# Splitting the gate weights of a top-2 dispatch by group: the second group's logits and weights moved

## The chip, the cores and the metric

One Trainium2 chip, one of its cores. The time is device microseconds of one execution, median of three runs: 240.18 us (239.93 to 241.43). No matrix work is done; what matters are the 16 DMA engines of the core, which carry all transfers, VectorE, a little of ScalarE, and the two queues from which transfers are issued (SyncE's and ScalarE's).

## The reference

For 16 x 1024 = 16384 tokens there is a row `x` of 512 floats and a row of 8 router logits. The softmax over the 8 is taken, the two largest probabilities are kept and divided by their sum, and the output holds each token's row twice, times the smaller and times the larger weight.

```python
probs = np.exp(router_logits - logits_max)
probs = probs / np.sum(probs, axis=-1, keepdims=True)
topk_indices = np.argsort(probs, axis=-1)[..., -k:]
topk_probs = np.take_along_axis(probs, topk_indices, axis=-1)
topk_probs = topk_probs / np.sum(topk_probs, axis=-1, keepdims=True)
x_expanded = x[:, :, np.newaxis, :].repeat(k, axis=2)
return (x_expanded * topk_probs[..., np.newaxis]).astype(np.float32)
```

All is float32. `x` is 33.6 MB, the logits 0.5 MB, the output 67.1 MB.

## The kernel before, in words

**Tiling.** A token is a row; the tokens are cut into two groups, 65 and 63 rows for each of the 128 partitions (`GROUPS`, L42). In each partition a group's rows are contiguous in memory, so a load of n rows is 128 pieces of n x 2 KB, and a store of n rows 128 pieces of n x 4 KB.

**Memory.** Four tiles of one buffer each: `xs` (65 rows of 512), into which rows are loaded and, once used, products are written too; `osp` (18 double rows), which holds only products; `WA` with the two weights of all 128 rows, and `dlt`. The weights' scratch and the logits lie in `osp` too (`room`, L102 to 107), before it takes its first product.

**Weights.** With two kept probabilities that are divided by their sum, the weights are the sigmoid of minus and plus the difference of the two largest logits. `top2_weights` (L14 to 38) finds the two largest with a tournament of maxima and minima: two steps on VectorE that pair logits 0 to 3 with 4 to 7 (L26, L27), four that halve this (L31 to 34), four that halve it again, and the difference (L36). ScalarE then takes two sigmoids (L37, L38) into `WA`. In the kernel before it is called once, for all 128 rows, so its VectorE steps are 512, 256 and 128 elements wide per partition.

**Order.** Everything is written out by hand, and transfers are kept in the order of the program on their queue. SyncE's queue issues for the first group loads of 2 and 4 rows, then the two groups' logits (L130 for 260 KB, L131 for 252 KB), then loads of 28 and 31 rows (`LOADS`, L44; issued at L122). The products (L138) follow in the order of `STORES` (L47): one `tensor_tensor` on VectorE multiplies n rows, each read twice, with their weights; it goes to `osp` or over rows of `xs` that have been used. Behind each product its store is issued (L151): the very first, of 3 rows, from ScalarE's queue, all others from SyncE's. The product that comes back to the start of `osp` is cut in two (`again`, `FREE`, L136 and 137), so that its first part waits for the small first store alone. The loads of the second group (16, 16 and 31 rows) stand in SyncE's queue behind the last store of the first group; each of them waits until the store that reads its place in `xs` is done. A last instruction of SyncE (L155) waits for the weights, the last product, and all transfers in `moved` but the last.

Of the kernel before, what the change touches and what calls it, by code (L numbers as in the profile page):

```python
# [1 line left out]

# [4 lines left out]

F32 = mybir.dt.float32
ALU = mybir.AluOpType
ACTF = mybir.ActivationFunctionType  # L10
P = 128


def top2_weights(nc, WA, dlt, room, logits, E):  # L14

    tt = nc.vector.tensor_tensor
    hi, lo, n = None, None, E  # L20
    while n > 1:
        n //= 2
        if hi is None:
            a, b = logits[:, :, 0:n], logits[:, :, n : 2 * n]
            nhi, nlo = room(n), b
            tt(nhi, a, b, op=ALU.max)  # L26
            tt(nlo, a, b, op=ALU.min)  # L27
        else:
            a, b = hi[:, :, 0:n], hi[:, :, n : 2 * n]
            nhi, nlo, tmp = room(n), room(n), room(n)  # L30
            tt(tmp, lo[:, :, 0:n], lo[:, :, n : 2 * n], op=ALU.max)  # L31
            tt(nlo, a, b, op=ALU.min)  # L32
            tt(nlo, nlo, tmp, op=ALU.max)  # L33
            tt(nhi, a, b, op=ALU.max)  # L34
        hi, lo = nhi, nlo
    tt(dlt, hi[:, :, 0], lo[:, :, 0], op=ALU.subtract)  # L36
    nc.scalar.activation(WA[:, :, 0], dlt, ACTF.Sigmoid, scale=-1.0)  # L37
    return nc.scalar.activation(WA[:, :, 1], dlt, ACTF.Sigmoid, scale=1.0)  # L38

GROUPS = [65, 63]  # L42

LOADS = [[2, 4, 28, 31], [16, 16, 31]]  # L44
BASE = [0, 1]

STORES = [  # L47
    [(0, 3, "osp", 0), (3, 15, "osp", 3), (18, 16, "xs", 0), (34, 15, "osp", 0), (49, 16, "xs", 33)],
    [(0, 16, "osp", 2), (16, 16, "xs", 0), (32, 15, "osp", 0), (47, 16, "xs", 32)],
]  # L50

L = 18

FREE = [3, 2]


@with_exitstack
def kernel(
    ctx: ExitStack,
    tc: tile.TileContext,  # L60
    x: bass.AP,
    router_logits: bass.AP,
    k: bass.AP,
    out: bass.AP,
):
    nc = tc.nc
    B, S, D = x.shape
    E = router_logits.shape[-1]
    N = B * S
    assert int(k) == 2 and E == 8 and N == P * sum(GROUPS)  # L70
    M = N // P

    x_v, o_v, rl_v = [], [], []
    t0 = 0
    for n in GROUPS:
        t1 = t0 + P * n
        x_v.append(
            x.rearrange("b s d -> (b s) d")[t0:t1].rearrange("(p m) d -> p m d", p=P)
        )
        o_v.append(  # L80
            out.rearrange("b s k d -> (b s) k d")[t0:t1].rearrange(
                "(p m) k d -> p m k d", p=P
            )
        )
        rl_v.append(
            router_logits.rearrange("b s e -> (b s) e")[t0:t1].rearrange(
                "(p m) e -> p m e", p=P
            )
        )
        t0 = t1  # L90

    wpool = ctx.enter_context(tc.tile_pool(name="wpool", bufs=1))
    xs = wpool.tile([P, max(GROUPS), D], F32)
    osp = wpool.tile([P, L, 2, D], F32)
    WA = wpool.tile([P, M, 2], F32)
    dlt = wpool.tile([P, M], F32)


    flat = osp.rearrange("p l k d -> p (l k d)")
    taken = [0]  # L100

    def room(n):  # L102
        o = taken[0]
        taken[0] += M * n
        return flat[:, o : o + M * n].rearrange("p (m n) -> p m n", n=n)

    logits = room(E)

    def place(where, at, n):

        if where == "osp":
            return osp[:, at : at + n]
        return xs[:, at : at + 2 * n, :].rearrange("p (r k) d -> p r k d", k=2)

    moved = []
    m0 = 0
    for g, G in enumerate(GROUPS):
        x0, r = BASE[g], 0
        for n in LOADS[g]:
            moved.append(  # L120
                tc.keep_in_program_order(
                    nc.sync.dma_start(  # L122
                        xs[:, x0 + r : x0 + r + n, :], x_v[g][:, r : r + n, :]
                    )
                )
            )
            r += n
            if g == 0 and r == 6:
                n0 = GROUPS[0]
                tc.keep_in_program_order(nc.sync.dma_start(logits[:, :n0], rl_v[0]))  # L130
                tc.keep_in_program_order(nc.sync.dma_start(logits[:, n0:], rl_v[1]))  # L131
                weights = top2_weights(nc, WA, dlt, room, logits, E)
        assert r == G
        for r, n, where, at in STORES[g]:
            og = place(where, at, n)
            again = where == "osp" and at == 0 and r > 0  # L136
            for a, b in [(0, FREE[g]), (FREE[g], n)] if again else [(0, n)]:
                product = nc.vector.tensor_tensor(  # L138
                    og[:, a:b],
                    xs[:, x0 + r + a : x0 + r + b, :]  # L140
                    .unsqueeze(2)
                    .to_broadcast([P, b - a, 2, D]),
                    WA[:, m0 + r + a : m0 + r + b, :]
                    .unsqueeze(3)
                    .to_broadcast([P, b - a, 2, D]),
                    op=ALU.mult,
                )

            queue = nc.scalar if g == r == 0 else nc.sync
            moved.append(  # L150
                tc.keep_in_program_order(queue.dma_start(o_v[g][:, r : r + n], og))  # L151
            )
        m0 += G

    seen = tc.keep_in_program_order(nc.sync.nop())  # L155
    for ins in [weights, product] + moved[:-1]:
        tc.add_manual_dep(
            seen.ins,
            ins.ins.name,
            mybir.DependencyInfo(  # L160
                mybir.DependencyClass.Sync, mybir.DependencyReason.DATA
            ),
            reason="all but the last transfer is done",
        )


# [1 line left out]
_INS = ['x', 'router_logits', 'k']  # L168
_OUTS = [((16, 1024, 2, 512), 'float32')]

_NUMBERS = {'k': 2}


# [26 lines left out]
```

## Time and profile before

| | before |
|---|---|
| median of three runs | 240.18 us |
| profiled execution, its own time | 241.36 us |
| span of the profiled execution | 239.6 us |
| bytes read, written | 34.08 MB, 67.11 MB |
| VectorE instructions | 22 |
| product of 16 rows (128x16384) | 17,224 ns |
| the weights' VectorE steps, first to last | 8.54 to 12.43 us |

The span runs from the first to the last instruction; the profiled execution's own time is 1.8 us longer. Times within the profile count from the start of the span. A transfer's row gives the time from its issue on the queue to its landing, so the time it stands behind earlier transfers is in it. The DMA share is the mean busy share of the 16 DMA engines; as packets of up to 64 KB are counted where they start, it swings above and below 1 in short windows and is to be read over long ones. "Idle before" an instruction, with the releaser, says for how long its engine stood still and what ended that.

### The profile page before, as it was taken

What the parts mean: (1) busy time and instruction counts of PE and PEld (TensorE: products, weight loads), DVE (VectorE), ACT (ScalarE), POOL (GpSimd) and SP (SyncE); (2) the same over time, 40 slices, a digit from 0 to 9 for tenths busy, and PEclk for the clock granted to TensorE, in tenths of its full rate; (3) what the DMA queues carried; (4) which work ended last, traced back from release to release, by engine and by line L of the source; (5) the groups of instructions that cost most, each with busy time, mean ns of one, the idle gap of its engine ahead of it and who ended that gap; (6) DMA issues with size and microseconds to landing.
All of it is one profiled execution on the core that took longest, in us unless ns stands there. A gap on an engine that the chain in (4) does not pass through costs nothing.

```text
span 239.6 us, 106 instructions
## 1 busy us (share of the span) xinstructions
DVE 141.9 (59%) x22; ACT 1.8 (1%) x3; POOL 0.2 (0%) x4
## 2 busy tenths in 40 slices
DVE  0560499999789999200000699999405999960000
ACT  2000000000000000000000000000000000000000
POOL 0000000000000000000000000000000000000000
DMA  7989998979989897999899999999999899898984
GB/s 253 528 373 483 427 415 376 493 339 492 481 372 492 383 482 339 482 437 449 361 421 438 438 438 498 435 419 471 405 405 471 372 503 442 380 492 360 514 350 186
DMA packets 2592, 101.19 MB, mean 422 GB/s; under 512 B 288, under 2 KB 416, under 8 KB 672
## 3 DMA queue, kind: packets, MB, share of 16 engines
q1 hardware_dynamic: 2448, 99.62, 96.7%
q10 hardware_dynamic: 144, 1.57, 1.5%
HBM read 34.08 MB, written 67.11 MB: 422 GB/s over the span
## 4 chain that ended last, share of the span: by engine, by line
DMA 48%; DVE 40%; SPq 1%; issue 0%; DVEq 0%
DMA xs<-in_x_dram 25%; DVE osp L138 25%; DMA out_dram<-osp 23%; DVE xs L138 14%; SPq L122 0%; SPq L131 0%; SPq L130 0%; SPq L151 0%; DVEq L138 0%
## 5 line engine op out<-in xcount | busy, mean ns | idle before, releaser
L138 DVE TENSOR_TENSOR osp<-xs,WA 128x3072 f32<-128x3072 f32 (+5 forms) x7 | 69.4, 9909 | 62.7 <-DMA xs<-in_x_dram 47.3
L138 DVE TENSOR_TENSOR xs<-xs,WA 128x16384 f32<-128x16384 f32 x4 | 68.9, 17224 | 0.1
L26 DVE TENSOR_TENSOR osp<-osp 128x512 f32<-128x512 f32 x1 | 0.7, 693 | 8.5 <-DMA osp<-in_router_logits_dram 8.5
L37 ACT ACT_TABLE_LOAD x1 | 1.3, 1283 | 0.7 <-PEq L181 0.7
L27 DVE TENSOR_TENSOR osp<-osp 128x512 f32<-128x512 f32 x1 | 0.7, 691 | 0.0
L32 DVE TENSOR_TENSOR osp<-osp 128x256 f32<-128x256 f32 (+1 forms) x2 | 0.7, 351 | 0.0
L31 DVE TENSOR_TENSOR osp<-osp 128x256 f32<-128x256 f32 (+1 forms) x2 | 0.7, 350 | 0.0
L34 DVE TENSOR_TENSOR osp<-osp 128x256 f32<-128x256 f32 (+1 forms) x2 | 0.7, 350 | 0.0
L33 DVE TENSOR_TENSOR osp<-osp 128x256 f32<-128x256 f32 (+1 forms) x2 | 0.7, 350 | 0.0
L37 ACT ACTIVATE WA<-dlt 128x128 f32<-128x128 f32 x1 | 0.3, 315 | 10.5 <-DVE dlt L36 10.5
L36 DVE TENSOR_TENSOR dlt<-osp 128x128 f32<-128x128 f32 x1 | 0.3, 292 | 0.0
L38 ACT ACTIVATE WA<-dlt 128x128 f32<-128x128 f32 x1 | 0.3, 297 | 0.0
L181 POOL MEMSET const-bfloat16-1.0<- 128x1 bf16 x1 | 0.1, 101 | 0.0
L181 POOL MEMSET const-uint8-127<- 128x1 uint8 x1 | 0.1, 101 | 0.0
L181 POOL MEMSET const-float32-0.0<- 128x1 f32 x1 | 0.1, 98 | 0.2 <-issue 0.2
L181 POOL MEMSET const-float32-1.0<- 128x1 f32 x1 | 0.1, 98 | 0.0
## 6 DMA issues: line engine op xcount, KB each, us to landing
out_dram<-osp SPq DMA_DIRECT2D x3, 7680.0 KB, 23.5
xs<-in_x_dram SPq DMA_DIRECT2D x2, 7936.0 KB, 42.2
xs<-in_x_dram SPq DMA_DIRECT2D x2, 4096.0 KB, 40.1
xs<-in_x_dram SPq DMA_DIRECT2D x1, 7168.0 KB, 24.8
out_dram<-osp ACTq DMA_DIRECT2D x1, 1536.0 KB, 26.6
xs<-in_x_dram SPq DMA_DIRECT2D x1, 1024.0 KB, 5.9
xs<-in_x_dram SPq DMA_DIRECT2D x1, 512.0 KB, 3.9
osp<-in_router_logits_dram SPq DMA_DIRECT2D x1, 260.0 KB, 6.2
```

What stands on the lines that cost most here:

```text
L26: tt(nhi, a, b, op=ALU.max)
L27: tt(nlo, a, b, op=ALU.min)
L31: tt(tmp, lo[:, :, 0:n], lo[:, :, n : 2 * n], op=ALU.max)
L32: tt(nlo, a, b, op=ALU.min)
L33: tt(nlo, nlo, tmp, op=ALU.max)
L34: tt(nhi, a, b, op=ALU.max)
L36: tt(dlt, hi[:, :, 0], lo[:, :, 0], op=ALU.subtract)
L37: nc.scalar.activation(WA[:, :, 0], dlt, ACTF.Sigmoid, scale=-1.0)
L38: return nc.scalar.activation(WA[:, :, 1], dlt, ACTF.Sigmoid, scale=1.0)
L138: product = nc.vector.tensor_tensor(og[:, a:b], xs[:, x0 + r + a : x0 + r + b, :] .unsqueeze(2) .to_broadcast([P, b - a, 2, D]), WA[:, m0 ...
L181: nc = _bacc.Bacc("TRN2", target_bir_lowering=False, num_devices=1)
```

## The change

`top2_weights` is called once for each group, on the group's part of `WA` and `dlt`, so its steps are 260, 130 and 65 elements wide for the first group and 252, 126 and 63 for the second. The first group's logits still lie in `osp` and are loaded behind the 2 and 4 rows. The second group's logits go to a tile of their own, `late`, and their load is issued between those of 28 and 31 rows. The second group's weights stand, on VectorE, between the last product of the first group and the first of the second. Their scratch is again the start of `osp`, which the store of rows 34 to 48 of the first group has read before. Each of SyncE's transfers is still there, 18 transfers in all; both logits loads are now in `moved`, and both pairs of sigmoids are waited for at the end.

```diff
+    late = wpool.tile([P, GROUPS[1], E], F32)
     flat = osp.rearrange("p l k d -> p (l k d)")
-    taken = [0]
-
-    def room(n):
-        o = taken[0]
-        taken[0] += M * n
-        return flat[:, o : o + M * n].rearrange("p (m n) -> p m n", n=n)
-
-    logits = room(E)
+    moved, weights = [], []
+
+    def weigh(g):
+
+        n, m = GROUPS[g], sum(GROUPS[:g])
+        taken = [0]
+
+        def room(e):
+            o = taken[0]
+            taken[0] += n * e
+            return flat[:, o : o + n * e].rearrange("p (m n) -> p m n", n=e)
+
+        logits = room(E) if g == 0 else late
+        if g == 0:
+            fetch(g, logits)
+        weights.append(
+            top2_weights(nc, WA[:, m : m + n], dlt[:, m : m + n], room, logits, E)
+        )
+
+    def fetch(g, logits):
+        moved.append(tc.keep_in_program_order(nc.sync.dma_start(logits, rl_v[g])))
...
     for g, G in enumerate(GROUPS):
         x0, r = BASE[g], 0
+        if g == 1:
+            weigh(1)
         for n in LOADS[g]:
...
             r += n
             if g == 0 and r == 6:
-                n0 = GROUPS[0]
-                tc.keep_in_program_order(nc.sync.dma_start(logits[:, :n0], rl_v[0]))
-                tc.keep_in_program_order(nc.sync.dma_start(logits[:, n0:], rl_v[1]))
-                weights = top2_weights(nc, WA, dlt, room, logits, E)
+                weigh(0)
+            if g == 0 and r == 34:
+                fetch(1, late)
...
-    for ins in [weights, product] + moved[:-1]:
+    for ins in weights + [product] + moved[:-1]:
```

More of the change, by code (lines that the diff above doesn't have):

```diff
@@ L113, in place @@
         return xs[:, at : at + 2 * n, :].rearrange("p (r k) d -> p r k d", k=2)
-    moved = []
     m0 = 0
```

## The prediction, before the result was known

> **What bounds the kernel now.** I read the page's first three parts, then windows over the stream of transfers, then the queue's own waits, then the order of time and the transfers one by one. The profiled execution took 241.36 us, its span is 239.6, so 1.8 us lie around it; the median of the three runs shown is 240.18. The sum below is made against the 241.36 and carried over to the median, which lies 1.2 us lower; the changed kernel's time will be a median too.
>
> ```profile
> DVE 141.9 (59%) x22; ACT 1.8 (1%) x3; POOL 0.2 (0%) x4
> DMA packets 2592, 101.19 MB, mean 422 GB/s; under 512 B 288, under 2 KB 416, under 8 KB 672
> q1 hardware_dynamic: 2448, 99.62, 96.7%
> q10 hardware_dynamic: 144, 1.57, 1.5%
> DMA 48%; DVE 40%; SPq 1%; issue 0%; DVEq 0%
> ```
>
> VectorE is busy 59% of the span; the two transfer queues together hold the 16 DMA engines for 98.2% of it. The span windows say where the other 1.8% is:
>
> ```profile
> 0.00:2.00 2.00, 0.00 (x0) 1.28 (x1) 0.20 (x4) 1.00 0.25 31
> 2.00:236.00 234.00, 141.92 (x22) 0.52 (x3) 0.00 (x0) 1.00 1.00 432
> 236.00:239.60 3.60, 0.00 (x0) 0.00 (x0) 0.00 (x0) 1.00 0.04 18
> ```
>
> The last two columns are the DMA share and GB/s. From 2 to 236 us the share is 1.00 at 432 GB/s: 234 us x 432 GB/s = 101.1 MB, all that is moved. Outside there are 2.0 us of start and 3.6 of end. So the time is the bytes over one rate, and the profile's chain of waits, which walks through VectorE for 40% of the span, only shows in what order the stream was fed. A change gains only if it takes bytes or a gap out of the stream, and loses only if it makes one. The test is therefore the cover: how long the stream still has work when the next transfer is issued.
>
> ```profile
> 0.72 0.85 SPq L122 DMA_DIRECT2D xs<-in_x_dram  x2
> 1.62 0.42 SPq L130 DMA_DIRECT2D osp<-in_router_logits_dram  x1
> 2.09 0.43 SPq L131 DMA_DIRECT2D osp<-in_router_logits_dram  x1
> 2.56 1.14 SPq L122 DMA_DIRECT2D xs<-in_x_dram  x2
> 8.54 0.69 DVE L26 TENSOR_TENSOR osp<-osp 128x512 f32<-128x512 f32 x1 [8.54 <-DMA osp<-in_router_logits_dram]
> 12.14 0.29 DVE L36 TENSOR_TENSOR dlt<-osp 128x128 f32<-128x128 f32 x1
> 13.02 3.36 DVE L138 TENSOR_TENSOR osp<-xs,WA 128x3072 f32<-128x3072 f32 x1 [0.58 <-ACT WA L38]
> 16.40 0.37 ACTq L151 DMA_DIRECT2D out_dram<-osp  x1
> 27.42 16.16 DVE L138 TENSOR_TENSOR osp<-xs,WA 128x15360 f32<-128x15360 f32 x1 [11.04 <-DMA xs<-in_x_dram]
> 43.60 0.35 SPq L151 DMA_DIRECT2D out_dram<-osp  x1
> 67.08 12.96 DVE L138 TENSOR_TENSOR osp<-xs,WA 128x12288 f32<-128x12288 f32 x1 [2.98 <-DMA out_dram<-osp]
> 80.07 0.33 SPq L151 DMA_DIRECT2D out_dram<-osp  x1
> 97.33 0.33 SPq L151 DMA_DIRECT2D out_dram<-xs  x1
> 133.58 17.22 DVE L138 TENSOR_TENSOR osp<-xs,WA 128x16384 f32<-128x16384 f32 x1 [36.28 <-DMA xs<-in_x_dram]
> 150.83 0.34 SPq L151 DMA_DIRECT2D out_dram<-osp  x1
> ```
>
> Each row is start and length. The transfers' own rows give KB and us from issue to landing (the first line is the 512 KB load issued at 0.72, the 7680 KB one the store of 43.60, the 24.4 that of 80.07, the 31.2 that of 150.83):
>
> ```profile
> xs<-in_x_dram SPq DMA_DIRECT2D x1, 512.0 KB, 3.9
> osp<-in_router_logits_dram SPq DMA_DIRECT2D x1, 260.0 KB, 6.2
> osp<-in_router_logits_dram SPq DMA_DIRECT2D x1, 252.0 KB, 6.4
> xs<-in_x_dram SPq DMA_DIRECT2D x1, 7168.0 KB, 24.8
> xs<-in_x_dram SPq DMA_DIRECT2D x1, 7936.0 KB, 45.6
> out_dram<-osp ACTq DMA_DIRECT2D x1, 1536.0 KB, 26.6
> out_dram<-osp SPq DMA_DIRECT2D x1, 7680.0 KB, 23.5
> out_dram<-osp SPq DMA_DIRECT2D x1, 7680.0 KB, 24.4
> out_dram<-osp SPq DMA_DIRECT2D x1, 31.2
> ```
>
> The store of 43.60 is the tightest. Its 7.86 MB are 18.2 us at 432 GB/s; it lands after 23.5, so it waited or was in latency for 5.3 us. The 512 KB load, the first in an empty queue, took 3.9 us of which 1.2 are bytes, so an estimate of issue latency plus completion is 2.7. The cover there is 5.3 - 2.7 = 2.6 us; at 80.07 it is 24.4 - 18.2 - 2.7 = 3.5, and at 150.83 (8.39 MB, 19.4 us) 31.2 - 19.4 - 2.7 = 9.1.
>
> **The change part by part.** Logits load of group two, 252 KB, moved from before the 28-row load to behind it. Bytes: the same, 0.26 MB, 0.60 us at 432 GB/s. Ahead of the 28 rows they are gone, so that load's issue goes from 2.56 to about 2.09 and it lands up to 0.6 us sooner. The 31-row load stays the sixth issue of the queue with the same bytes before it, so its landing, and with it the place where stores begin, moves by 0. The target is a new tile, same row length. A small load standing between two large ones is not shown in the trace before; the nearest rows are the two logits loads, which landed at 1.62 + 6.2 = 7.8 and 2.09 + 6.4 = 8.5, 0.7 us apart for 0.60 us of bytes. Bounds: -0.6 (all that the earlier landing could give) to +0.1 beyond the bytes, paid before as well; I take 0.
>
> First group's weights. They wait for one small load, not two: from 8.54 to about 7.8. The chain from 8.54 to the end of L36 at 12.43 takes 3.9 us with widths 512, 256 and 128:
>
> ```profile
> L26 DVE TENSOR_TENSOR osp<-osp 128x512 f32<-128x512 f32 x1 | 0.7, 693 | 8.5 <-DMA osp<-in_router_logits_dram 8.5
> L32 DVE TENSOR_TENSOR osp<-osp 128x256 f32<-128x256 f32 x1 | 0.4, 419 | 0.0
> L32 DVE TENSOR_TENSOR osp<-osp 128x128 f32<-128x128 f32 x1 | 0.3, 283 | 0.0
> L37 ACT ACTIVATE WA<-dlt 128x128 f32<-128x128 f32 x1 | 0.3, 315 | 10.5 <-DVE dlt L36 10.5
> ```
>
> That is 1.06 ns per element and some 150 ns beside: 260 wide about 425 ns, 130 wide 285, 65 wide 215. Two of the first, four and four of the others and one of 220 are 3.1 us busy where before there were 693 + 691 + 4 x 418 + 4 x 282 + 292 = 4.5; their starts follow each other some 80 ns closer than that, so the chain takes about 2.4 us (between half of 3.9 and 3.9). The first product starts at about 13.02 - 0.7 - 1.5 = 10.8, and the first store is issued at about 14.2, not 16.40. On the path this is 0: what the next product waits for at 27.42 is the 28-row load, and the stream is full.
>
> What an earlier first store does to the 28 rows. It shares the engines with them. 1.57 MB in 26.6 us is 0.06 MB per us, so 2.2 us more of it are 0.13 MB, 0.3 us: the 28 rows land at 27.4 - 0.6 + 0.3 = 27.1, and the store of 43.60 goes out near 43.3, with more cover. The bad end: all 1.57 MB, 3.6 us, before the 28 rows finish, and none of it before: +3.6 - 0.6 = 3.0, less 2.6 of cover, leaves 0.4 us at the end of the span. I take 0, as the row's own rate is nearer. The Trainium skill, page "DMA: Bandwidth & Descriptors", section on queues, rings and completion order, says that each engine alternates between queues packet by packet; no row here shows single turns, and by that rule the store takes about one more turn before the 28 rows end, again well inside the cover, so the sum would be the same 0, unless the little logits packets pair with the store's and let it finish by about 30 us instead of 43, which nobody waits for.
>
> Second group's weights. Eleven VectorE steps more than before in all and two of ScalarE, 2.4 us plus at most 0.6 (two like the 315 ns row). Their first step has a new wait: scratch is the tile of the store issued at 80.07, which lands at 80.07 + 24.4 = 104.5, so they run not right behind the last product, whose store goes out at 97.33, but from 104.5 to about 107.5. Queued behind them on VectorE is the product of 133.58, which waits for rows until then anyway: 26 us of cover. Behind that, if it were gone, stands the 9.1 us of cover of the store at 150.83; only past both would the 3.0 us count. ScalarE's queue holds nothing after the first store; SyncE issues nothing more or less than before (the logits' issue of 0.43 us only changes places). Cost 0.
>
> Sum: 241.36 + 0 for the profiled execution, 240.2 for the median.
>
> **The rivals.** (1) The head passes on: the logits out of the way and the weights earlier shift everything behind. The chain of waits speaks for it, since it runs from the 28-row load through the product of 27.42 to the store of 43.60. The full share against it. It gives 240.2 - 0.6 = 239.6 by the load, at most 240.2 - 2.2 = 238.0 if the 2.2 us of the first store came through whole. (2) The slower side: the small load breaks the stream between the two large ones, since the engines must set it up and finish it. Its price is the 2.7 us of latency of the 512 KB row, in the head before hidden in the ramp: 240.2 + 2.7 = 242.9. It decides as soon as the DMA share between 25 and 32 us falls clearly under 1. The two small loads 0.7 us apart speak against it. The Trainium skill, same page, section "Anatomy of one DMA", puts a DMA's fixed cost at about 2.0 us (for the software path), mostly waiting for completion; if that stopped the stream, the time would be 242.2, and by the 0.7 us the trace does not agree that it does. (3) The change doesn't do what it says: the second weights wait for a store later than I read, and delay the product of 133.58. Price nothing until 26 + 9.1 us are used up, then 3.0: 243.2.
>
> **How the numbers follow.** Forecast 0.85, rival 1 0.08, rival 2 0.05, rival 3 0.02. The range starts from 239.93 and 241.43, the ends of the runs shown, whose spread of 1.5 us is larger than any term: less 0.6 below (the load's gain) is 239.3, and 241.5 above takes in the highest run, with the bad end's 240.6 well inside. About 1% (2.4 us) is what a measurement of this kernel can tell from no change. Only the extreme of rival 1 comes near it from below, 0.03 with what I can't see; above it lie rivals 2 and 3, and part of rival 2 stays inside: 0.05. Within 1%: 0.92.
>
> **What would show it.** Right: DMA share 1.00 at 432 GB/s from 2 to 236 us again; first weights step near 7.8 us, first store issued near 14; 28 rows landing at 26.8 to 27.5; store before 43.6; eleven small VectorE steps between about 104 and 108, DVE busy near 141.9 - 4.5 + 2 x 3.1 = 143.6 with 33 instructions; the product after them again ended by the load near 133.5, and the last store issued near 213. Wrong: a window under 0.95 around 25 to 32 or at 44 to 50, or a VectorE wait for ScalarE's weights at 133. The forecast falls if a transfer's rate itself changes with the order, which no row of one execution can tell.

## The result, and the profile after

The changed kernel takes 241.1 us (median of 15 runs, 240.36 to 243.0) against 240.03 (15 runs, 239.82 to 241.43): a ratio of 1.0051, 95% interval 1.0036 to 1.0066. That is 1.2 us by the ratio and 1.1 by the medians, inside the range and inside "within 1%", but a small loss and not nothing. Run again beside the kernel before on another occasion it gave 1.0060 (1.0035 to 1.0085).

The page of the changed kernel answers to the rows that carried the prediction:

```profile
DVE 143.0 (60%) x33; ACT 2.1 (1%) x5; POOL 0.2 (0%) x4
q1 hardware_dynamic: 2448, 99.62, 96.8%
q10 hardware_dynamic: 144, 1.57, 1.5%
DMA 48%; DVE 40%; SPq 1%; issue 0%; DVEq 0%
```

Eleven VectorE instructions more, 1.1 us more of VectorE (the prediction had 143.6 in place of 143.0), the same packets and bytes. The windows (last two columns: DMA share, GB/s):

```profile
0.00:2.00 2.00, 0.00 (x0) 1.27 (x1) 0.20 (x4) 1.00 0.22 25
2.00:236.00 234.00, 142.96 (x33) 0.82 (x5) 0.00 (x0) 1.00 1.01 432
236.00:240.00 4.00, 0.00 (x0) 0.00 (x0) 0.00 (x0) 1.00 0.04 16
```

The stream is as full as before. Of the two shorter windows that were to stay above 0.95, the one from 25 to 32 us does (0.96 before, 1.12 after). The one from 44 to 50 us doesn't; this is its row before and then after:

```profile
44.00:50.00 6.00, 6.00 (x1) 0.00 (x0) 0.00 (x0) 1.00 1.14 477
44.00:50.00 6.00, 5.96 (x2) 0.00 (x0) 0.00 (x0) 1.00 0.81 343
```

It is no hole. The window counts a packet where it starts; if each packet is counted for the part of it that lies between 44 and 50 us, the engines are busy for 1.00 of that time in both kernels. The order of time (start, length):

```profile
7.69 0.43 DVE L26 TENSOR_TENSOR osp<-osp 128x260 f32<-128x260 f32 x1 [7.69 <-DMA osp<-in_router_logits_dram]
9.98 0.23 DVE L36 TENSOR_TENSOR dlt<-osp 128x65 f32<-128x65 f32 x1
14.07 0.37 ACTq L165 DMA_DIRECT2D out_dram<-osp  x1
27.85 16.16 DVE L152 TENSOR_TENSOR osp<-xs,WA 128x15360 f32<-128x15360 f32 x1 [13.81 <-DMA xs<-in_x_dram]
44.04 0.35 SPq L165 DMA_DIRECT2D out_dram<-osp  x1
80.50 0.33 SPq L165 DMA_DIRECT2D out_dram<-osp  x1
104.93 0.42 DVE L26 TENSOR_TENSOR osp<-late 128x252 f32<-128x252 f32 x1 [7.20 <-DMA out_dram<-osp]
107.60 0.24 ACT L38 ACTIVATE WA<-dlt 128x63 f32<-128x63 f32 x1
134.03 17.23 DVE L152 TENSOR_TENSOR osp<-xs,WA 128x16384 f32<-128x16384 f32 x1 [26.62 <-DMA xs<-in_x_dram]
151.28 0.34 SPq L165 DMA_DIRECT2D out_dram<-osp  x1
```

The product that waits for the 28 rows starts at 27.85, where it was 27.42, and from there on everything is 0.4 us later: 44.04 for 43.60, 80.50 for 80.07, 134.03 for 133.58, and the span 240.0 for 239.6. In these rows nothing is added behind 28 us. So the place to look at is the 28-row load and its neighbours; KB and us from issue to landing:

```profile
xs<-in_x_dram SPq DMA_DIRECT2D x1, 7168.0 KB, 25.7
late<-in_router_logits_dram SPq DMA_DIRECT2D x1, 252.0 KB, 27.7
out_dram<-osp ACTq DMA_DIRECT2D x1, 1536.0 KB, 15.9
```

The 28 rows, issued at 2.10, take 25.7 us though 252 KB less stand before them. And the first store, issued 2.3 us earlier, lands 13 us earlier, at 14.07 + 15.9 = 30.0, not 43.0.

The trace also holds every packet's start and length; a packet here is one of the 128 pieces. It doesn't name the packet's engine, but on one engine each packet starts where the one before it ended. A transfer of 128 pieces is 8 packets on each of 16 engines, and in this stream most packets of one size take the same time: 57,344 B (a piece of the 28-row load) 2116 ns, 98 of the 128 before and 92 after. The last one of each engine does not:

```
28-row load, packets     before  before again  after  after again
others, mean ns            2127          2124   2134         2138
last 16, mean ns           2533          2426   3133         3072
last 16, least to most  2334-2680   2214-2569  2995-3416  2922-3196
lost per engine, us        0.49          0.37   1.15         1.11
```

"Lost" is the sum over the 128 packets of what each takes beyond 2116 ns, divided by 16 engines. The change costs each engine 0.66 us there by the first two profiles, 0.74 by the second two. No other packet group differs by more than 0.13.

The profile of before shown above the prediction was of a long execution (241.36 us): one of its 16 engines ended its last store 2.0 us behind the middle ones. So was that of the changed kernel (241.74 us, one engine 1.6 us behind). A second profile of the same kernel has a span of 237.8 us, and beside it the changed kernel's second one, 239.0, shows the step without so late an engine. Before again:

```profile
26.81 16.16 DVE L138 TENSOR_TENSOR osp<-xs,WA 128x15360 f32<-128x15360 f32 x1 [10.66 <-DMA xs<-in_x_dram]
65.97 12.96 DVE L138 TENSOR_TENSOR osp<-xs,WA 128x12288 f32<-128x12288 f32 x1 [2.48 <-DMA out_dram<-osp]
211.66 0.33 SPq L151 DMA_DIRECT2D out_dram<-xs  x1
```

After again:

```profile
27.51 16.16 DVE L152 TENSOR_TENSOR osp<-xs,WA 128x15360 f32<-128x15360 f32 x1 [13.53 <-DMA xs<-in_x_dram]
67.05 12.96 DVE L152 TENSOR_TENSOR osp<-xs,WA 128x12288 f32<-128x12288 f32 x1 [2.85 <-DMA out_dram<-osp]
212.78 0.33 SPq L165 DMA_DIRECT2D out_dram<-xs  x1
```

0.70 us later at the 28 rows, 1.08 at the landing of the 15-row store (a transfer lands when its slowest of 16 engines is through), 1.12 at the last issue. These rows follow the slowest engine; the middle one of the 16 ends its last store 0.7 us later in both pairs (236.5 to 237.2 and 236.4 to 237.1, in the table below).

### The profile page after: what moved, and what is told of

Read it like the earlier page. It is cut to its first block, busy times and chain, and to the rows that moved or that the text cites. A ratio compares the mean times of both kernels' runs of the same rounds, so it can differ in the third digit from the quotient of the medians.

```text
span 240.0 us, 119 instructions
## 1 busy us (share of the span) xinstructions
DVE 143.0 (60%) x33; ACT 2.1 (1%) x5; POOL 0.2 (0%) x4
## 4 chain that ended last, share of the span: by engine, by line
DMA 48%; DVE 40%; SPq 1%; issue 0%; DVEq 0%
DMA xs<-in_x_dram 26%; DVE osp L152 25%; DMA out_dram<-osp 23%; DVE xs L152 14%; SPq L137 0%; SPq L121 0%; SPq L165 0%; DVEq L152 0%
## 5 line engine op out<-in xcount | busy, mean ns | idle before, releaser
L26 DVE TENSOR_TENSOR osp<-osp 128x260 f32<-128x260 f32 x1 | 0.4, 430 | 7.7 <-DMA osp<-in_router_logits_dram 7.7
L37 ACT ACTIVATE WA<-dlt 128x65 f32<-128x65 f32 (+1 forms) x2 | 0.5, 260 | 105.0 <-DVE dlt L36 105.0
L34 DVE TENSOR_TENSOR osp<-osp 128x130 f32<-128x130 f32 (+3 forms) x4 | 1.0, 254 | 0.0
L33 DVE TENSOR_TENSOR osp<-osp 128x130 f32<-128x130 f32 (+3 forms) x4 | 1.0, 253 | 0.0
L32 DVE TENSOR_TENSOR osp<-osp 128x130 f32<-128x130 f32 (+3 forms) x4 | 1.0, 252 | 0.0
L31 DVE TENSOR_TENSOR osp<-osp 128x130 f32<-128x130 f32 (+2 forms) x3 | 0.7, 243 | 0.0
L36 DVE TENSOR_TENSOR dlt<-osp 128x65 f32<-128x65 f32 (+1 forms) x2 | 0.5, 227 | 0.1
L38 ACT ACTIVATE WA<-dlt 128x65 f32<-128x65 f32 (+1 forms) x2 | 0.5, 244 | 0.0
L27 DVE TENSOR_TENSOR osp<-osp 128x260 f32<-128x260 f32 x1 | 0.4, 428 | 0.0
## 6 DMA issues: line engine op xcount, KB each, us to landing
xs<-in_x_dram SPq DMA_DIRECT2D x1, 7168.0 KB, 25.7
out_dram<-osp ACTq DMA_DIRECT2D x1, 1536.0 KB, 15.9
```

## The experiments

Theory A: the small load right behind the 28-row load, while the first store shares the engines, holds the engines up. Theory B: the earlier first store does it. Rivals were added as the runs came. Times are medians of 12 runs (15 for the first profiles of before and after, 5 and 6 where said), ratios are to the kernel before on the same chip. The table is worked out from the packets of each profile: "28" and "31" are the us lost per engine in the loads of 28 and 31 rows of the first group (where the 31 rows are cut, in the largest part), "31b" in the 31-row load of the second; "middle" and "last" are where the middle and the last engine end their last store, in us from the start; "lowest" is the shortest run.

```
run                 28    31    31b   middle  last   lowest  median  ratio (95%)
before             0.49  0.21  0.09  236.5   238.5  239.82  240.03
before again       0.37  0.04  0.14  236.4   236.7  239.55  239.74  0.9986 (0.9970-1.0002)
after              1.15  0.08  0.17  237.2   238.8  240.36  241.10  1.0051 (1.0036-1.0066)
after again        1.11  0.07  0.14  237.1   237.9  240.41  241.61  1.0060 (1.0035-1.0085)
e1_behind31        0.83  0.00  0.15  236.5   239.5  239.74  240.32  1.0025 (0.9999-1.0052)
e2_head            0.59  0.15  0.20  236.5   237.0  239.67  239.91  1.0007 (0.9983-1.0031)
e3_store_sync      0.01  1.25  0.05  236.9   237.3  240.13  240.28  1.0010 (0.9995-1.0024)
e4_store_late      1.39  0.00  0.11  237.0   238.3  240.40  240.98  1.0039 (1.0009-1.0069)
e5_store_second    0.00  0.05  0.62  236.8   237.5  239.90  240.66  1.0019 (0.9996-1.0043)
e6_cut_1_30        1.05  0.02  0.07  237.1   237.4  240.23  240.71  1.0021 (1.0002-1.0041)
e7_cut_16_15       0.57  0.00  0.92  237.8   239.4  241.55  241.86  1.0069 (1.0042-1.0096)
e8_late_on_act     0.54  0.10  0.17  236.6   238.0  239.83  240.99  1.0031 (1.0006-1.0056)
e9_store_behind28  0.00  0.76  0.09  236.6   238.9  241.14  241.78  1.0082 (1.0052-1.0112)
e10_cut_1_1_29     1.08  0.03  0.13  237.2   237.7  240.39  240.68  1.0030 (1.0016-1.0043)
```

**The small load moved on, behind the 31 rows.**

```diff
-            if g == 0 and r == 34:
+            if g == 0 and r == 65:
                 fetch(1, late)
```

> The changed kernel with the second logits' load issued behind the 31-row load, not before it; the first store still goes out early, near 14.1 us. Theory A (the small load right behind the 28-row load, while the first store shares the engines, holds the engines up): the last packets of the 28-row load are no slower than before the change, the 28 rows land near 27.2 us, and the time is that of before, 240.0 to 240.3. Theory B (it is the earlier first store that slows the 28-row load): the time stays at that of the changed kernel, near 241.1, and the 28 rows land near 27.8.

240.32 us, lowest 239.74. The lowest runs and the middle engine (236.5) are those of before, as A says. The median lies between, because 3 of 12 runs are over 241. The profiled run was one of these (242.37 us): its 28 rows lost 0.83 and landed near 28.6, later than B would have it, with one engine 3.0 us behind the middle one. Its last packets speak for A all the same: they average 2606 ns, or 2536 without a single one of 3653, where before they took 2533. The rest of the loss lies in earlier packets.

**The small load where it was before, all else as changed.**

```diff
                 weigh(0)
-            if g == 0 and r == 34:
-                fetch(1, late)
+                fetch(1, late)
```

> The changed kernel with the second logits' load issued where it was before the change, ahead of the 28-row load; weights are still split by group and the first store still goes out near 14.1 us. Theory A (small load behind the 28-row load): 240.0 to 240.3. Theory B (earlier first store): near 241.1. If the second group's weights at 105 us cost anything, it shows here too, as something above 240.3 with a landing of the 28 rows no later than 27.5.

239.91 us, 1.0007 (0.9983 to 1.0031), lowest 239.67: the loss is gone, with the first store still out at 13.81 and the second group's weights still computed from 103.6 us. Within that interval this clears the split of the weights, the new tile and the earlier store at once.

**The first store from SyncE's queue.**

```diff
-            queue = nc.scalar if g == r == 0 else nc.sync
+            queue = nc.sync
```

> The changed kernel with the first store (3 rows) issued from SyncE's queue behind the 31-row load, so that no second queue shares the engines with the loads. Theory A and B both need that sharing: the slow last packets of the 28-row load go, the 28 rows land near 25.5, and the time is 240.0 or lower (the packets that were slow before the change, some 0.5 us, are saved as well: 239.5). If the slow packets belong to the loads themselves and not to the sharing, the time stays near 241.1.

240.28 us, 1.0010 (0.9995 to 1.0024). Without a store beside it the 28-row load loses 0.01, though the small load still stands behind it. But the loss is not saved: the last packets of the 31-row load, which now have the store's short packets behind them, lose 1.25. The hoped 239.5 is a miss.

**The first store as late as before, the small load where the change put it.**

```diff
                 weigh(0)
+                row = xs[:, 0:5, :]
+                spare = osp[:, 5:8].rearrange("p l k d -> p (l k) d")
+                nc.vector.tensor_tensor(spare[:, 0:5, :], row, row, op=ALU.max)
```

> The changed kernel with one more VectorE step of 2560 elements in unused scratch before the first group's weights, so that the first store goes out near 16.2 us as before the change, while the second logits' load stays between those of 28 and 31 rows. Theory A (small load behind the 28-row load): near 241.1, as the changed kernel. Theory B (earlier first store): 240.0 to 240.3.

240.98 us with the store issued at 15.91 (16.40 before the change) and 1.39 lost in the 28 rows, 1.01 of it in the last packets. B falls: the time of the store's issue isn't what matters.

**The first store behind the 15-row store.** The loop holds the first product's store back and issues it on SyncE's queue after the next one.

```diff
-            queue = nc.scalar if g == r == 0 else nc.sync
...
+            if g == r == 0:
+                first = og
+                continue
+            for q, m, o in [(r, n, og)] + ([(0, 3, first)] if g == 0 and r == 3 else []):
```

> The changed kernel with the first store (3 rows) issued from SyncE's queue behind the 15-row store. No store then stands directly behind the 28-row load or beside it, and behind the 31-row load stands a store of 60 KB packets as before the change, not one of 12 KB packets. Theory A, as the runs so far leave it (the last packets of a load are slow where short packets of stores come up directly behind them; 0.5 us lost before the change, 1.15 after): load of 28 rows without slow packets, that of 31 with 0.1 to 0.2 us of them, so 239.2 to 239.6, under both kernels. Rival (slow packets are lost at the first turn from loads to stores wherever it is, as in the run with the first store behind the 31-row load): 240.2 to 240.4. Third outcome: the products that go back to the start of the small tile wait for the later store, and the stream breaks: over 240.5.

240.66 us, lowest 239.90. Both loads of the first group lose next to nothing (0.00 and 0.05), as A says, and yet the time isn't lower: 0.62 is lost in the last load of the second group and 0.3 in a store before it. A's gain is a miss. In this run the loss left its place and as much was lost elsewhere. Behind the slow packets of the second group's load there come only a store's packets of 65,536 B, so short packets are not the only thing that goes with a slow last packet.

**The kernel before with one row cut off the 31.** It has none of the change's parts but a small load in the same place.

```diff
-LOADS = [[2, 4, 28, 31], [16, 16, 31]]
+LOADS = [[2, 4, 28, 1, 30], [16, 16, 31]]
```

> The kernel before the change, logits in their old places, with the 31-row load cut into loads of 1 and of 30 rows: 128 pieces of 2 KB stand behind the 28-row load as after the change, with none of its other parts. Theory A: as slow as the changed kernel, near 241.0, with 1 us or more on each engine's last packet of the 28-row load. Rival (the logits themselves, their new tile or the split of the weights): 239.9 to 240.2.

240.71 us, 1.0021 (1.0002 to 1.0041); 1.05 lost in the 28 rows, lowest 240.23. This is the clearest pair: the first store is issued as before, and lands like the changed kernel's. The profile of this kernel:

```profile
16.23 0.37 ACTq L151 DMA_DIRECT2D out_dram<-osp  x1
27.50 16.16 DVE L138 TENSOR_TENSOR osp<-xs,WA 128x15360 f32<-128x15360 f32 x1 [11.30 <-DMA xs<-in_x_dram]
```

```profile
out_dram<-osp ACTq DMA_DIRECT2D x1, 1536.0 KB, 14.1
xs<-in_x_dram SPq DMA_DIRECT2D x1, 256.0 KB, 27.3
```

16.23 + 14.1 = 30.3 for the store's landing, where the kernel before had 16.40 + 26.6 = 43.0, and 27.50 for the product, where before again had 26.81: 0.69 us later, and the packets of the 28 rows lost 1.05 - 0.37 = 0.68 more.

**The same load cut into two large ones.**

```diff
-LOADS = [[2, 4, 28, 31], [16, 16, 31]]
+LOADS = [[2, 4, 28, 16, 15], [16, 16, 31]]
```

> The kernel before the change with the 31-row load cut into loads of 16 and 15 rows, that is one load more, none of them small. Theory A: 239.9 to 240.2, as before the change, since pieces of 32 KB keep the store's short packets apart. Rival (any additional load behind the 28-row load costs it): near 241.0.

241.86 us (5 runs, lowest 241.55): a miss. The 28 rows lose 0.57, as A says, so what it says of its own place holds; the time alone can't tell A from its rival, which had 241.0. But 0.92 is lost in the second group's last load and 0.48 in the store of 97 us. Why a cut at 30 us does this at 120 and 158 was not found.

**The small load on ScalarE's queue, behind the first store.**

```diff
-            if g == 0 and r == 34:
-                fetch(1, late)
...
+            if g == r == 0:
+                fetch(1, late)
```

> The changed kernel with the second logits' load issued from ScalarE's queue behind the first store, so that SyncE's queue goes from the 28-row load straight to the 31-row load. Theory A: 239.9 to 240.2, last packets of the 28-row load slow by no more than before the change. Rival (a small load among the large ones costs wherever it is): near 241.0.

240.99 us, lowest 239.83; 0.54 lost in the 28 rows and the middle engine at 236.6, so A is right on the packets. The median is a miss, and it is the rival's (near 241.0): 6 of 12 runs are over 241. The packets and the lowest run are against the rival; the scatter is not explained by A.

**The first store only when the small load is nearly through.** Four of the spare VectorE steps of above put it off to 23.62.

```diff
+                for _ in range(4):
+                    nc.vector.tensor_tensor(spare[:, 0:5, :], row, row, op=ALU.max)
```

> The changed kernel with four more VectorE steps of 2560 elements in unused scratch around the first group's weights, so that the first store goes out near 24 us, from ScalarE's queue as before, when the 28-row load and the small load behind it are nearly through. Theory A (the small load costs because the first store's short packets run beside it): no slow packets of the 28-row load, and the lowest runs fall back from those of the changed kernel (240.4) to 239.6 or lower; median 239.5 to 240.2. Rival (the small load behind the 28-row load costs by itself): lowest runs near 240.4, median near 241. Second rival (the loss moves to the next turn from loads to stores): slow packets of the 31-row load instead, 240.2 to 240.6.

241.78 us (6 runs, lowest 241.14). No 28-row packet is slow (0.00), so the small load behind it costs nothing by itself; this part of A holds. The time is a miss, and worse than any that was named: the store now runs beside the whole 31-row load, which loses 0.76, and one engine ends 2.3 us behind the middle one. All six runs are over 241; that the store's place is the reason is not shown.

**Two small loads.**

```diff
-LOADS = [[2, 4, 28, 31], [16, 16, 31]]
+LOADS = [[2, 4, 28, 1, 1, 29], [16, 16, 31]]
```

> The kernel before the change with the 31-row load cut into loads of 1, 1 and 29 rows: two small loads behind the 28-row load. Theory A as a loss that is paid once, when the first store's packets come up together behind the 28-row load: as with one small load, lowest runs near 240.2, median 240.7 to 241.0. Rival (a price for each small load): lowest runs near 240.9, median near 241.5.

240.68 us, 1.08 lost: the same as with one (240.71). The loss is paid once, and not for each small load.

**Both kernels once more.** No edit.

> The kernel before the change once more, for a second profile of it: 239.9 to 240.2. Theory A: last packets of the 28-row load slow by 0.4 to 0.6 us per engine again.

> The changed kernel once more, beside the kernel before on the same chip, for a second profile: 240.7 to 241.3, ratio 1.002 to 1.006. Theory A: last packets of the 28-row load slow by 1.0 to 1.4 us per engine again. If the first profile was an odd one, by 0.4 to 0.6.

239.74 and 241.61 us, 0.37 and 1.11 lost in the 28 rows: the first profiles were no odd ones. 7 of 12 runs of the changed kernel are over 241, none of these 12 of the kernel before.

## Why the prediction came out as it did

The time that bounds the kernel was read rightly: bytes over 432 GB/s, from 2 to 236 us, before and after. No gap opened between transfers where cover was counted. The second group's weights ran from 104.93 to 107.84 (predicted 104.5 to 107.5), and the product behind them was again ended by its rows, at 134.03. Moving these weights is worth nothing in either direction, which the run with the small load in its old place shows apart from everything else (1.0007). The first weights step came at 7.69 (predicted 7.8), the first store at 14.07 (14.2), and that helped nobody, as said. VectorE's 143.6 us was 0.6 too high because the steps' durations were added though they overlap (a chain took 2.5 us, not 3.1); nothing hung on it.

The step that failed is the first one: "I take 0" for the load's new place, with bounds of -0.6 to +0.1 beyond its bytes. It costs some 0.7 us. The 2.6 us of cover at the store of 43.60 don't hide this: cover hides a late issue, and here the engines' own time is spent in longer packets, so the rows from 27.85 on all come later. The rows I took the bound from, two small loads 0.7 us apart in the head, stand behind another load with no store beside them, and there a small load is indeed free: the run with the first store at 23.62 has no slow packet in front of it either. With the store's short packets waiting in the other queue it isn't. This is rival 2 in its place and sign, held at 0.05, though with 0.7 us and not the 2.7 of a broken stream. The hole that I named as its mark isn't there (the 0.81 from 44 to 50 us comes from where packets are counted): in the changed kernel's profile the packets are longer, and a busy share of 1 hides that. That the time still lies in the range is in part luck. The range took its ends from the spread of the runs shown, not from a term for this loss, and 241.1 is near its upper end of 241.5.

With it fell the 27.1 us for the landing of the 28 rows (27.83, outside the 26.8 to 27.5 named as the sign of being right), whose 0.6 us of gain is eaten by the slow packets, and the store that was to go out before 43.6 went out at 44.04.

The sentence on the Trainium skill came nearest. By the Trainium skill's rule of turns between queues (page "DMA: Bandwidth & Descriptors", section on queues, rings and completion order) the little packets would pair with the store's and let it finish by about 30 us; it landed at 30.0, so the trace agrees. I went on that nobody waits for that store, which is true, and missed that such a run of short packets has a price at the packet before it.

The 1.2 us aren't explained to the end. The kernels that differ from before by a small load alone have medians 0.7 and 0.8 us above it (240.71 with one against 240.02, 240.68 with two against 239.92; by the ratios 0.5 and 0.7), which is what the packets of the 28 rows show. The rest, 0.3 to 0.5 us of median, is scatter: 16 of 27 runs of the changed kernel are over 241 us. Of the kernel before it is 2 of 15 and 0 of 12, and 11 of 92 in its runs beside the experiments, so it has such runs too, but fewer. The small load alone doesn't bring them (3 of 24 in the two kernels just named), nor does the rest of the change (2 of 12 with the small load in its old place); with both together and the first store late it is 6 of 12, and with the small load on ScalarE's queue 6 of 12 as well. In the profiled executions of 241.36 us and more one engine of 16 ends 1.6 to 3 us behind the middle one. What makes that likelier after the change stays open. So does the mechanism inside an engine: shown is that the last packet of the 28-row load grows by some 0.6 us more when a run of short packets comes up behind it, not why; and in two runs (the first store behind the 15-row store, the load cut into 16 and 15 rows) the last packets of another load grew with no such run of short packets behind them.

## What to carry to other kernels

In a stream that keeps all transfer engines busy, ask of a moved transfer not only what hides it but what stands beside it in the other queue: a load of 2 KB pieces dropped behind a load of 57 KB pieces cost 0.7 us while a store of 12 KB pieces waited, and no slow packet without that store. A busy share of 1 doesn't prove that nothing is lost; compare the lengths of packets of one size. And before a profile is used as the base, see where it stands among the runs: the first one here was 1.2 us above the median of three runs, with one engine late.

## What the runs showed of the hardware that was not expected

- Packets of the large stores take the same time nearly to the nanosecond (61,440 B 2267 ns in 383 of 384 packets before, 65,536 B 2418 in 634 of 640), whether VectorE works beside them or not. In the loads it is mostly the last packet of each engine that is longer: of the 28-row load's loss it held 0.42 of 0.49 us before and 1.02 of 1.15 after, and a single one was up to 1.3 us longer.
- When such a loss is cleared in one place, one can turn up in another. Taking the store from beside the 28-row load cleared it there (1.15 to 0.01) and left 1.25 at the end of the 31-row load; with the store behind the next one, 0.62 turned up 115 us later. That it is the same loss that moves is not shown.
- A store that shares engines with a load goes one packet against one: the 1.5 MB store took 26.6 us beside 57 and 62 KB packets and 14 to 16 us when 2 KB packets came in between.
